# Forward and backward state steps of a chunked linear attention in one VectorE operation, on one core of a Trainium2 chip

## The chip, the core and the metric

The kernel runs on one core of one Trainium2 chip. The core has five engines that run their own queues in order and meet through semaphores: TensorE (PE in the profile, with its weight loads shown as PEld), VectorE (DVE), ScalarE (ACT), GpSimd (POOL) and SyncE (SP, which here only issues transfers). Matrix products go to PSUM, eight banks of 2 KB in each of 128 rows; everything else works in SBUF. The metric is the device time of one execution in microseconds (us), as the median of several runs.

## The reference

One layer of an encoder on x of 1024 positions by 1024 features, all in float32:

```python
h = rmsnorm(x, norm_mix_pre);  y = mixer(h, ...);      x = x + rmsnorm(y, norm_mix_post)
h = rmsnorm(x, norm_ffn_pre);  y = conv_mlp(h, ...);   x = x + rmsnorm(y, norm_ffn_post)
```

The mixer projects h once and splits the columns into a short convolution branch (y_a) and a gated linear attention (y_b) of four heads, with 64 key and 128 value features, run once forward and once backward over the positions. For one head and one direction, in chunks of 64 positions:

```python
cum = cumsum(log_a, within a chunk);  cum_last = cum at the chunk's end
q_in, k_in, k_out = q*exp(cum), k*exp(-cum), k*exp(cum_last - cum)
o_intra = mask(q_in @ k_in.T) @ v
kv      = k_out.T @ v                       # 64 x 128 for each of 16 chunks
state_(n+1) = exp(cum_last)_n * state_n + kv_n          # the chain over chunks
o       = o_intra + q_in @ state_n
```

The backward direction does the same on flipped inputs, with gates of its own. The outputs of both directions are added, normalised over each head's 128 features, multiplied with silu of a gate, joined with y_a and multiplied with w_out. conv_mlp is an up projection to 2 x 2816, a width-3 convolution over positions, a gated product and a down projection.

## The kernel before, in words

Weights and activations of the large products are split into a rounded part (names ending in h) and a remainder (l), and each product is three TensorE passes. Four of the large projections use a block scheme that needs seven block products in place of eight; its sums of weight blocks are made by GpSimd ahead of time, from rows of w_up and w_down that it loads itself, and are written back to DRAM (wud, wup, wdd) for the second half of the kernel. One such job is `up_begin`/`up_end` (tiles wu0 to wu3), `down_begin`/`down_end` (tiles wd0r, wd1r, ... two a job) or `pair_begin`/`pair_end` (wp4, wp5). A job's begin loads two tiles of 512 KB; its end makes four operations of 128x512 (L108 to L111, or L146 to L149, called sums in this text) and stores the tiles. `side()` takes the next job from a list: it begins it and ends what has been begun, all but the newest `ahead` jobs.

The order of work is that in which a scheduler lays out the program's operations; each engine then runs its list strictly in order. The part around the change is the attention heads, from 118 to 345 us of the span. There TensorE alternates between two kinds of work, head by head: projections of the convolution branch (pgc, pgv, pgb, 48 passes of 128x512 each) and of the next head's q and k (pqk), which keep it busy, and between them the attention products of one head: pko (the transpose of the decayed keys, tile `cum`), kv (k_out times v, L727), sc (scores, L708), po (outputs, L782 and L785) and pot (the transpose of the normalised outputs, L802). Between the passes of a projection, a list called `between` slips in pko, kv and sc of a head.

In SBUF, the first 64 rows of a head's tiles belong to the forward direction and the last 64 to the backward one: S (the states of 16 chunks, 128 columns each), dec (the decay of each chunk), qd, kin and cum. For a head:

- ScalarE copies kv from PSUM to S, four copies for each half of the chunks (L735 for the forward rows, L739 for the backward rows). The state that enters chunk c lies in S[:, c] for both directions, so the forward chain runs upward in c and the backward chain downward.
- `scan` then runs the chain on VectorE: 14 steps of 64 rows forward (`step_f`, L744) and 14 of 64 rows backward (`step_b`, L748), alternating in the middle. Its operations stand in VectorE's list together with the masking of the scores (L711, L715, giving A), the convolution branch (c, u, yT), the remainders of weights (L219), and the gates of the next head (m, cum, cl, L665 to L685).
- TensorE makes po in one PSUM tile of two banks: first 16 products of A with v, each with 64 rows and 64 output rows (L782), then 16 products of qd with S that take all 128 rows at once and so add both directions (L785).
- ScalarE squares po into `on` (L792), VectorE reduces it (L793), a few short operations make the factor, and VectorE multiplies po with it into `on` (L795). TensorE transposes `on` into pot, and VectorE writes yT (L803).

Between a head's reduce and the next head's kv copies, ScalarE's list holds the factor's two operations (L197, L199), a weight's rounding (L218), two copies of q (L651, L652) and the copy of pko to koT (L696), which the next kv products read.

PSUM tiles come from a pool of four tiles of two banks; a tile's first write waits for the last reader of the one that had its banks. The jobs' tiles come from a pool of eight (tag y) that also holds the yT tiles.

The main loop calls, for each head h, the attention's steps and the convolution's steps in turn, and `side()` once before the first head, and once after the heads 0 and 1.

Of the kernel before, what the change touches and what calls it, by code (L numbers as in the profile page):

```python
# [16 lines left out]
P = 128  # L17
# [23 lines left out]
def kernel(  # L41
# [39 lines left out]
    def ps_tile(name):  # L81
        return psp.tile([P, 1024], F32, tag="ps", name=name)
# [78 lines left out]

    begun, loads = [], []

    def side(tile=row_tile, after=None, ahead=0):


        if jobs:
            begin, end, i = jobs.pop(0)
            begun.append((end, i, begin(i, tile, after)))
        while len(begun) > ahead:  # L170
            end, i, t = begun.pop(0)
            with tc.issue_after(loads[-1].ins) if ahead else ExitStack():
                end(i, *t)

    NPB = 21
# [456 lines left out]


    S = mp.tile([P, NC, DV], F32, tag="S", name="S")
    nc.vector.memset(S[0:DK, 0, :], 0.0)
    nc.vector.memset(S[DK:P, NC - 1, :], 0.0)

    last_act = [None]
    left = []
    copied, gated = {}, [None]  # L640

    def gla_head(h):
# [31 lines left out]
        nc.vector.tensor_copy(cl[0:DK], cumv[0:DK, :, CH - 1])  # L674
        nc.vector.tensor_copy(cl[DK:P], cumv[DK:P, :, 0])
        s = 1.0 / 16.0
        nc.scalar.activation(dec, cl, AF.Exp, scale=s)
        kin = unit("kin", f"kin{h}")
        nc.scalar.activation(m, cum, AF.Exp, scale=s)
        nc.scalar.activation(kin, cum, AF.Exp, scale=-s)  # L680
# [36 lines left out]
        def states(i):  # L717
            b = i // 2
            if i % 2 == 0:
                tiles["kv"] = ps_tile(f"kv{h}_{b}")  # L720
            kv = tiles["kv"]
            for c8 in range(4 * (i % 2), 4 * (i % 2) + 4):
                t = b * 4 + c8 // 2
                par = c8 % 2
                r = slice(par * CH, (par + 1) * CH)
                o0 = par * HALF + (c8 // 2) * DV
                nc.tensor.matmul(kv[:, o0 : o0 + DV], tiles["koT"][r, t * P : (t + 1) * P], V[t][r, h * DV : (h + 1) * DV],  # L727
                                 start=True, stop=True)
            if i % 2 == 0:
                return  # L730
            kvv = kv.rearrange("p (a i d) -> p a i d", a=2, d=DV)
            for par in range(2):
                lo_c = b * 8 + par
                n = 4 if lo_c + 6 + 1 <= NC - 1 else 3
                nc.scalar.copy(S[0:DK, lo_c + 1 : lo_c + 1 + 2 * n - 1 : 2, :], kvv[0:DK, par, 0:n, :])  # L735
                i0 = 1 if lo_c == 0 else 0
                c0 = lo_c + 2 * i0
                n = 4 - i0
                last_act[0] = nc.scalar.copy(S[DK:P, c0 - 1 : c0 - 1 + 2 * n - 1 : 2, :], kvv[DK:P, par, i0:4, :])  # L739
            if b == 1:  # L740
                scan()

        def step_f(c):
            nc.vector.scalar_tensor_tensor(S[0:DK, c + 1, :], S[0:DK, c, :], dec[0:DK, c : c + 1], S[0:DK, c + 1, :],  # L744
                                           op0=ALU.mult, op1=ALU.add)

        def step_b(c):
            nc.vector.scalar_tensor_tensor(S[DK:P, c - 1, :], S[DK:P, c, :], dec[DK:P, c : c + 1], S[DK:P, c - 1, :],  # L748
                                           op0=ALU.mult, op1=ALU.add)

        def scan():
            for c in range(1, 8):
                step_f(c)
            for i in range(8, 15):
                step_b(NC + 6 - i)
                step_f(i)
            for c in range(7, 0, -1):
                step_b(c)

        def all_states():  # L760

# [6 lines left out]
        between.extend((decayed, lambda: None, all_states, lambda: None, lambda: [scores(i) for i in range(4)]))  # L768
        yield

        po = ps_tile(f"po{h}")

        for inner in (True, False):
            for c in range(NC) if inner else (c for g in range(0, NC, 4) for c in (g, g + 2, g + 1, g + 3)):
                t, par = divmod(c, 2)
                o0 = par * HALF + t // 2 * DV
                o = po[t % 2 * CH : (t % 2 + 1) * CH, o0 : o0 + DV]
                if inner:  # L780
                    r = slice(par * CH, (par + 1) * CH)
                    nc.tensor.matmul(o, A[r, t * CH : (t + 1) * CH], V[t][r, h * DV : (h + 1) * DV],  # L782
                                     start=t < 2, stop=False, skip_group_check=True)
                else:
                    nc.tensor.matmul(o, qd[:, c * CH : (c + 1) * CH], S[:, c, :], start=False, stop=True,  # L785
                                     skip_group_check=True)
        on = unit("sq", f"on{h}")
        ov = on.rearrange("p (t d) -> p t d", d=DV)
        ss = small.tile([P, NT], F32, tag="ssh", name=f"ssh{h}", bufs=2)

        with tc.high_priority() if h == 0 else ExitStack():
            nc.scalar.activation(on, po, AF.Square)  # L792
            nc.vector.reduce_sum(out=ss, in_=ov, axis=mybir.AxisListType.X)  # L793
            rs = rstd_of(ss, DV)
            nc.vector.tensor_mul(ov, po.rearrange("p (t d) -> p t d", d=DV), rs.unsqueeze(2).to_broadcast([P, NT, DV]))  # L795
        yield

        def outputs():
# [658 lines left out]
```

## Time and profile before

| | |
|---|---|
| median of 3 runs | 1069.47 us (1068.31 to 1071.57) |
| the profiled execution's own time | 1070.88 us |
| its span, first to last instruction | 1069.1 us, 14218 instructions |
| TensorE busy (matmul) | 1042.1 us (97%) |
| VectorE busy | 844.9 us (79%) |
| ScalarE busy | 480.0 us (45%) |
| GpSimd busy | 295.6 us (28%) |
| mean granted TensorE clock | 0.989 |

In a timeline row stand the start in us from the span's start, the time it took, engine, line and operation, then tiles and shapes as output<-input, the count of merged instructions, and in brackets the engine's idle time before it with what ended it. A row of merged instructions has the time from the first one's start to the last one's end. In the view of waits a row gives who waited, for whom, the total in us, how often, and the longest. In the view of stretches a row gives the stretch, its length, each engine's busy time with its number of instructions, the granted clock, the DMA share and GB/s.

### The profile page before, as it was taken

Reading aid. Unit: us, or ns where it says so; the run is one execution under the profiler, and the core shown is the slowest. Engines: PE = TensorE matmul, PEld = TensorE weight load, DVE = VectorE, ACT = ScalarE, POOL = GpSimd, SP = SyncE. Lnnn points to the kernel's source line nnn. Section 1 sums busy time; section 2 is a strip of 40 time slices with the busy share of each in tenths; the row PEclk is TensorE's granted clock in tenths of the full one; section 3 lists DMA queues with packets and bytes.
Section 4 is the critical chain, followed back from the end, with each engine's and each line's share of the span. In section 5 each row is a group of like instructions: output and inputs, shape, how many; then the busy total and the mean of one; then the engine's idle time right before and its main releaser. Section 6 shows DMA issues by size and latency. Waiting matters only on the chain.

```text
span 1069.1 us, 14218 instructions
## 1 busy us (share of the span) xinstructions
PE 1042.1 (97%) x5385; PEld 871.2 (81%) x5385; DVE 844.9 (79%) x1037; ACT 480.0 (45%) x664; POOL 295.6 (28%) x274
## 2 busy tenths in 40 slices
PE   8999996899999999999999999999999999999997
PEld 7987884788888888887888888888888888888886
DVE  6884679798878887999979877977987886655476
ACT  6552481545444334744534434344444455343443
POOL 1434485300006840001322423342240007600001
PEclk9999997899999999999999999999999999999999
DMA  9201665201247864344423323223333579977555
GB/s 303 100 20 45 192 229 185 79 21 40 60 128 243 288 248 148 99 129 158 138 75 122 118 69 128 99 89 109 109 105 102 193 266 342 357 253 233 176 163 212
DMA packets 126599, 165.02 MB, mean 154 GB/s; under 512 B 16177, under 2 KB 83906, under 8 KB 126530
## 3 DMA queue, kind: packets, MB, share of 16 engines
q1 hardware_dynamic: 114802, 121.90, 35.6%
q0 software_dynamic: 11152, 40.38, 10.3%
q10 hardware_dynamic: 576, 1.84, 0.4%
q8 instruction: 42, 0.69, 0.3%
q14 instruction: 27, 0.22, 0.1%
HBM read 117.68 MB, written 46.40 MB: 153 GB/s over the span
## 4 chain that ended last, share of the span: by engine, by line
PE 87%; DVE 8%; ACT 2%; DMA 1%; issue 1%; POOL 0%; SPq 0%; DVEq 0%; POOLq 0%; ACTq 0%
PE pb L311 16%; PE pc L311 11%; PE pdb L1325 10%; PE pa L311 9%; PE pw L933 8%; PE pgc L260 4%; PE pv L453 4%; PE pgv L260 3%; PE pqk L260 3%; PE pdd L1325 3%; PE pdc L1325 3%; PE pda L1325 3%; PE pgb L260 2%; DVE S L744 1%; PE pdl L1325 1%; PE pga L311 1%
## 5 line engine op out<-in xcount | busy, mean ns | idle before, releaser
L1325 PE MATMUL pdb<-d 128*128 128x512 f32 (+1 forms) x495 | 109.5, 382 | 0.0
L1325 PEld LDWEIGHTS pdb<-d 128*128 128x128 f32 x495 | 90.7, 188 | 18.0
L311 PE MATMUL pb<-t,uv 128*128 128x512 f32 x264 | 63.4, 389 | 0.0
L311 PEld LDWEIGHTS pb<-t,uv 128*128 128x128 f32 x264 | 49.5, 188 | 10.3
L1208 DVE TENSOR_TENSOR cg<-cv,pb 128x512 f32<-128x512 f32 x22 | 15.0, 684 | 35.3 <-PE pb L311 18.1
L1256 ACT ACTIVATE uu<-uu 128x1024 f32<-128x1024 f32 x22 | 23.4, 1062 | 35.9 <-DVE uu L1178 35.9
L744 DVE SCALAR_TENSOR_TENSOR S<-S,dec 64x128 f32<-64x128 f32 x56 | 28.0, 500 | 12.2 <-ACT S L735 10.5
L1214 ACT COPY cg<-pa 128x512 f32<-128x512 f32 x22 | 12.9, 587 | 47.0 <-PE pa L311 47.0
L1068 POOL TENSOR_TENSOR us61r<-uv6r 128x512 f32<-128x512 f32 x1 | 1.7, 1737 | 110.5 <-DVE cv L1236 110.5
L123 POOL COPY wp5g<-ident 128x1 f32<-128x1 f32 x1 | 0.2, 206 | 115.0 <-PE pgc L260 115.0
L1177 DVE SCALAR_TENSOR_TENSOR uv<-cv,prm,uv 128x1023 f32<-128x1023 f32 x22 | 31.9, 1448 | 0.0
L1325 PE MATMUL pdc<-d 128*128 128x512 f32 x132 | 30.1, 389 | 0.0
L1325 PE MATMUL pdd<-d 128*128 128x512 f32 x132 | 30.1, 389 | 0.0
L1325 PEld LDWEIGHTS pdd<-d 128*128 128x128 f32 x132 | 24.8, 188 | 5.1
L1325 PEld LDWEIGHTS pdc<-d 128*128 128x128 f32 x132 | 24.8, 188 | 5.1
L1178 DVE SCALAR_TENSOR_TENSOR uu<-cg,prm,uu 128x1023 f32<-128x1023 f32 x22 | 28.9, 1312 | 0.0
L1376 POOL DMA_DIRECT2D x2r<-x2d x4 | 2.1, 531 | 95.5 <-DMA d_8r<-actd 84.8
L946 ACT ACTIVATE tmp<-x 128x1024 f32<-128x1024 f32 x8 | 8.5, 1061 | 44.0 <-DVE x L943 44.0
L1178 DVE SCALAR_TENSOR_TENSOR uv<-cv,prm,uv 128x1023 f32<-128x1023 f32 x22 | 28.0, 1274 | 0.0
L1177 DVE SCALAR_TENSOR_TENSOR uu<-cg,prm,uu 128x1023 f32<-128x1023 f32 x22 | 28.0, 1274 | 0.0
L1259 DVE TENSOR_TENSOR uu<-uu,uv 128x1024 f32<-128x1024 f32 x22 | 27.2, 1237 | 0.0
L1176 ACT ACTIVATE uu<-cg,prm 128x1024 f32<-128x1024 f32 x22 | 25.2, 1143 | 3.1 <-ACT uv L1176 1.9
(1268 smaller groups left out, 3285.0 us busy)
## 6 DMA issues: line engine op xcount, KB each, us to landing
actd<-as SPq DMA_DIRECT2D x20, 512.0 KB, 2.7
x<-in_x_dram SPq DMA_DIRECT2D x16, 512.0 KB, 6.2
actd<-uu SPq DMA_DIRECT2D x10, 512.0 KB
x2d<-x SPq DMA_DIRECT2D x8, 512.0 KB, 3.1
actd<-uu SPq DMA_DIRECT2D x10, 256.0 KB, 2.0
out_dram<-o POOLq DMA_DIRECT2D x5, 512.0 KB, 6.1
x2r<-x2d POOLq DMA_DIRECT2D x4, 512.0 KB, 4.9
x2r<-x2d SPq DMA_DIRECT2D x4, 512.0 KB, 4.2
```

Of the source, the lines that this page charges most:

```text
L260: nc.tensor.matmul(o[hf], wt[:, k, :], act[hf][a][:, k, :], start=(k == 0 and wt is wh and a == 0), stop=(k == KT - 1 and wt is wl))
L311: nc.tensor.matmul(o, w[:, k, :], m[:, k, :], start=start and k == 0 and q == 0, stop=k == 3 and q == 2, skip_group_check=True)
L453: keep(nc.tensor.matmul(ps[:, n * 512 : n * 512 + VH], a[:, k, sl], w[:, k % 2, n * VH : (n + 1) * VH], start=(j == 0), stop=(j == 3 * KT ...
L744: nc.vector.scalar_tensor_tensor(S[0:DK, c + 1, :], S[0:DK, c, :], dec[0:DK, c : c + 1], S[0:DK, c + 1, :], op0=ALU.mult, op1=ALU.add)
L933: ins = nc.tensor.matmul(ps[:, n * HALF : (n + 1) * HALF], a[:, k, sl], w[:, n * HALF : (n + 1) * HALF], start=(i == 0 and q == 0), stop=( ...
L1176: nc.scalar.activation(u, src, AF.Copy, scale=ffn_tap(1, r))
L1177: nc.vector.scalar_tensor_tensor(u[:, 1:L], src[:, 0 : L - 1], ffn_tap(0, r), u[:, 1:L], op0=ALU.mult, op1=ALU.add)
L1178: nc.vector.scalar_tensor_tensor(u[:, 0 : L - 1], src[:, 1:L], ffn_tap(2, r), u[:, 0 : L - 1], op0=ALU.mult, op1=ALU.add)
L1208: nc.vector.tensor_add(cg[:, hi], cv[:, lo], pb)
L1256: last_act[0] = nc.scalar.activation(ug, ug, AF.Silu)
L1259: nc.vector.tensor_mul(ug, ug, uv)
L1325: nc.tensor.matmul(o, a[:, 0, sl], b[:, 1, r], start=start and i == 0, stop=stop and i == 2, skip_group_check=True)
```

## The change

Four edits belong together.

1. The backward states are stored in S in reverse: the state that enters chunk c in the backward chain lies in S[64:128, 15 - c], and dec's backward half is reversed too (by a second ScalarE operation). Both chains then run upward, and one VectorE operation on 128 rows makes one step of both: 14 operations a head in place of 28. The zero that starts both chains is written by one operation.
2. Forward and backward states of one chunk no longer lie in the same column of S, so a product over 128 rows cannot take both. The products of qd with S are split: 16 for one half of the rows and 16 for the other, each with 64 rows. Together with the 16 products of A with v that makes 48 in three turns. The products that read rows 0 to 63 add into one PSUM tile (po...f), those that read rows 64 to 127 into another (po...b).
3. The evacuation adds the two: ScalarE copies the second tile to `on`, VectorE adds the first, ScalarE squares `on` into the first tile's banks, VectorE reduces from there, and the final product is made in place in `on`.
4. `side` takes a `hold`. In heads 0 and 1 GpSimd first copies one column of the last state (S[:, 15]) to a small tile (turn), and the ends of the jobs that are due stand behind that copy in its list. The call before the first head falls away; the job of wd2r and wd3r (wd1 in the prediction; the job of wd0r and wd1r is wd0 there) is only begun after head 0 and ends after head 1's steps, as do wp4's sums.

```diff
-    def side(tile=row_tile, after=None, ahead=0):
+    def side(tile=row_tile, after=None, ahead=0, hold=None):
...
-            with tc.issue_after(loads[-1].ins) if ahead else ExitStack():
+            with tc.issue_after(loads[-1].ins) if ahead else tc.issue_after(hold.ins) if hold else ExitStack():
                 end(i, *t)
...
-        nc.scalar.activation(dec, cl, AF.Exp, scale=s)
+        nc.scalar.activation(dec[0:DK], cl[0:DK], AF.Exp, scale=s)
+        nc.scalar.activation(dec[DK:P], cl[DK:P, ::-1], AF.Exp, scale=s)
...
-                c0 = lo_c + 2 * i0
+                c1 = NC - lo_c - 6
                 n = 4 - i0
-                last_act[0] = nc.scalar.copy(S[DK:P, c0 - 1 : c0 - 1 + 2 * n - 1 : 2, :], kvv[DK:P, par, i0:4, :])
+                last_act[0] = nc.scalar.copy(S[DK:P, c1 : c1 + 2 * n - 1 : 2, :],
+                                             kvv[DK:P, par, i0:4, :][:, ::-1, :])
             if b == 1:
-                scan()
...
+                for c in range(1, NC - 1):
+                    stepped[0] = nc.vector.scalar_tensor_tensor(S[:, c + 1, :], S[:, c, :], dec[:, c : c + 1],
+                                                                S[:, c + 1, :], op0=ALU.mult, op1=ALU.add)
...
-        po = ps_tile(f"po{h}")
+        po = [ps_tile(f"po{h}{x}") for x in "fb"]
...
+        for turn in range(3):
+            for c in range(NC):
                 t, par = divmod(c, 2)
...
+                d = par ^ (turn == 2)
+                r = slice(d * DK, (d + 1) * DK)
+                bank = (d, par, t % 2)
+                if turn == 0:
+                    w, v = A[r, t * CH : (t + 1) * CH], V[t][r, h * DV : (h + 1) * DV]
                 else:
+                    w, v = qd[r, c * CH : (c + 1) * CH], S[r, NC - 1 - c if d else c, :]
+                nc.tensor.matmul(out_of(c, d), w, v, start=bank not in seen, stop=turn > 0, skip_group_check=True)
...
-            nc.scalar.activation(on, po, AF.Square)
-            nc.vector.reduce_sum(out=ss, in_=ov, axis=mybir.AxisListType.X)
+            nc.scalar.copy(on, po[1])
+            nc.vector.tensor_add(on, on, po[0])
+            nc.scalar.activation(po[0], on, AF.Square)
+            nc.vector.reduce_sum(out=ss, in_=po[0].rearrange("p (t d) -> p t d", d=DV), axis=mybir.AxisListType.X)
...
     next(gla[0])
-    side()
     next(fill)
...
         next(fill)
+        if h < 2:
+
+            turn = small.tile([P, 1], F32, tag="ss", name=f"turn{h}")
+            side(hold=nc.gpsimd.tensor_copy(turn, S[:, NC - 1, 0:1]))
...
-        if h < 2:
-            side()
+        if h == 0:
+            side(ahead=1)
```

How GpSimd's list moves around head 0's steps. Before, from the last sum of wu2 on:

```order
L111 TENSOR_TENSOR wu2g<-wu2g 128x512
L108 TENSOR_TENSOR wu3v<-wu3v 128x512
L116 DMA wud<-wu2g 128x2x512
L140 DMA wd0r<-in_w_down_dram 128x1024
L109 TENSOR_TENSOR wu3v<-wu3g,wu3v 128x512
L140 DMA wd1r<-in_w_down_dram 128x1024
L110 TENSOR_TENSOR wu3g<-wu3v,wu3g 128x512
L115 DMA wud<-wu3v 128x2x512
L111 TENSOR_TENSOR wu3g<-wu3g 128x512
L146 TENSOR_TENSOR wd0r<-wd0r 128x512
```

and now:

```order
L111 TENSOR_TENSOR wu2g<-wu2g 128x512
L116 DMA wud<-wu2g 128x2x512
L140 DMA wd0r<-in_w_down_dram 128x1024
L140 DMA wd1r<-in_w_down_dram 128x1024
L851 COPY turn_1592<-S 128x1
L108 TENSOR_TENSOR wu3v<-wu3v 128x512
L146 TENSOR_TENSOR wd0r<-wd0r 128x512
L109 TENSOR_TENSOR wu3v<-wu3g,wu3v 128x512
L147 TENSOR_TENSOR wd0r<-wd1r,wd0r 128x512
L110 TENSOR_TENSOR wu3g<-wu3v,wu3g 128x512
L115 DMA wud<-wu3v 128x2x512
```

The eight sums of wu3 and wd0 stand behind the copy that reads the last state; the loads of wd0r and wd1r stay ahead of it.

VectorE's list of head 0 from the masking on. Before:

```order
L715 TENSOR_TENSOR A_1460<-Am 128x512
L748 SCALAR_TENSOR_TENSOR S<-S,dec_1313 64x128
L818 TENSOR_TENSOR c_1396<-c_1396,pgv_1467 128x1024
L748 SCALAR_TENSOR_TENSOR S<-S,dec_1313 64x128
L219 TENSOR_TENSOR gc1l<-gc1r,gc1h 128x1024
L748 SCALAR_TENSOR_TENSOR S<-S,dec_1313 64x128
L821 SCALAR_TENSOR_TENSOR u_1618<-c_1396,prm,u_1618 128x1023
L748 SCALAR_TENSOR_TENSOR S<-S,dec_1313 64x128
L822 SCALAR_TENSOR_TENSOR u_1618<-c_1396,prm,u_1618 128x1023
L665 TENSOR_SCALAR m_1630<-pg_1627,prm 128x1024
```

and now:

```order
L715 TENSOR_TENSOR A_1444<-Am 128x512
L744 SCALAR_TENSOR_TENSOR S<-S,dec_1312 128x128 x5
L813 TENSOR_TENSOR c_1380<-c_1380,pgv_1451 128x1024
L219 TENSOR_TENSOR gc1l<-gc1r,gc1h 128x1024
L664 TENSOR_SCALAR m_1618<-pg_1615,prm 128x1024
L816 SCALAR_TENSOR_TENSOR u_1588<-c_1380,prm,u_1588 128x1023
L667 TENSOR_TENSOR m_1618<-m_1618,cum_1619 128x1024
L817 SCALAR_TENSOR_TENSOR u_1588<-c_1380,prm,u_1588 128x1023
L668 SCALAR_TENSOR_TENSOR cum_1619<-rst,m_1618 64x1024
L669 SCALAR_TENSOR_TENSOR cum_1619<-rst,m_1618 64x1024
```

The last steps stand together ahead of the convolution branch, which before was woven with backward steps; lines below L634 have numbers smaller by one in the changed kernel, and those from L744 on shift by more. Further down in VectorE's list, the reduce of head 0 moves from ahead of the last product of the next head's gates to behind it. Before:

```order
L681 TENSOR_TENSOR cum_1631<-cl_1639,cum_1631 128x1024
L684 TENSOR_TENSOR kin_1644<-kin_1644,kd_1455 128x1024
L219 TENSOR_TENSOR gv1l<-gv1r,gv1h 128x1024
L793 TENSOR_REDUCE ssh_1743<-on_1742 128x8
L685 TENSOR_TENSOR cum_1631<-cum_1631,kd_1455 128x1024
L198 TENSOR_SCALAR rv<-ssh_1743,eps 128x8
```

and now:

```order
L681 TENSOR_TENSOR cum_1619<-cl_1627,cum_1619 128x1024
L684 TENSOR_TENSOR kin_1633<-kin_1633,kd_1439 128x1024
L219 TENSOR_TENSOR gv1l<-gv1r,gv1h 128x1024
L685 TENSOR_TENSOR cum_1619<-cum_1619,kd_1439 128x1024
L786 TENSOR_TENSOR on_1748<-on_1748,po0f 128x1024
L788 TENSOR_REDUCE ssh_1749<-po0f 128x8
L198 TENSOR_SCALAR rv<-ssh_1749,eps 128x8
```

The add of the two output tiles (L786) is new and stands between. TensorE's list keeps its order but for the 48 products in the place of 32.

More of the change, by code (lines that the diff above doesn't have):

```diff
@@ L634 @@
     S = mp.tile([P, NC, DV], F32, tag="S", name="S")
-    nc.vector.memset(S[0:DK, 0, :], 0.0)
-    nc.vector.memset(S[DK:P, NC - 1, :], 0.0)
-    last_act = [None]
+    nc.vector.memset(S[:, 0, :], 0.0)
+    last_act, stepped = [None], [None]
     left = []
@@ L736, in states @@
                 i0 = 1 if lo_c == 0 else 0
-                c0 = lo_c + 2 * i0
+                c1 = NC - lo_c - 6
                 n = 4 - i0
-                last_act[0] = nc.scalar.copy(S[DK:P, c0 - 1 : c0 - 1 + 2 * n - 1 : 2, :], kvv[DK:P, par, i0:4, :])
+                last_act[0] = nc.scalar.copy(S[DK:P, c1 : c1 + 2 * n - 1 : 2, :],
+                                             kvv[DK:P, par, i0:4, :][:, ::-1, :])
             if b == 1:
-                scan()
[L743 to L758, printed above, removed]
+                for c in range(1, NC - 1):
+                    stepped[0] = nc.vector.scalar_tensor_tensor(S[:, c + 1, :], S[:, c, :], dec[:, c : c + 1],
+                                                                S[:, c + 1, :], op0=ALU.mult, op1=ALU.add)
         def all_states():
@@ L769, in gla_head, with out_of @@
         yield
-        po = ps_tile(f"po{h}")
-        for inner in (True, False):
-            for c in range(NC) if inner else (c for g in range(0, NC, 4) for c in (g, g + 2, g + 1, g + 3)):
-                t, par = divmod(c, 2)
[L778 to L783, printed above, removed]
-                else:
-                    nc.tensor.matmul(o, qd[:, c * CH : (c + 1) * CH], S[:, c, :], start=False, stop=True,
-                                     skip_group_check=True)
+        po = [ps_tile(f"po{h}{x}") for x in "fb"]
+        def out_of(c, d):
+            t, par = divmod(c, 2)
+            o0 = par * HALF + t // 2 * DV
+            return po[d][t % 2 * CH : (t % 2 + 1) * CH, o0 : o0 + DV]
+        seen = set()
+        for turn in range(3):
+            for c in range(NC):
+                t, par = divmod(c, 2)
+                d = par ^ (turn == 2)
[3 more added lines that the diff above has]
+                    w, v = A[r, t * CH : (t + 1) * CH], V[t][r, h * DV : (h + 1) * DV]
+                else:
+                    w, v = qd[r, c * CH : (c + 1) * CH], S[r, NC - 1 - c if d else c, :]
+                nc.tensor.matmul(out_of(c, d), w, v, start=bank not in seen, stop=turn > 0, skip_group_check=True)
+                seen.add(bank)
         on = unit("sq", f"on{h}")
@@ L791, in gla_head @@
         with tc.high_priority() if h == 0 else ExitStack():
-            nc.scalar.activation(on, po, AF.Square)
-            nc.vector.reduce_sum(out=ss, in_=ov, axis=mybir.AxisListType.X)
+            nc.scalar.copy(on, po[1])
+            nc.vector.tensor_add(on, on, po[0])
+            nc.scalar.activation(po[0], on, AF.Square)
+            nc.vector.reduce_sum(out=ss, in_=po[0].rearrange("p (t d) -> p t d", d=DV), axis=mybir.AxisListType.X)
             rs = rstd_of(ss, DV)
-            nc.vector.tensor_mul(ov, po.rearrange("p (t d) -> p t d", d=DV), rs.unsqueeze(2).to_broadcast([P, NT, DV]))
+            nc.vector.tensor_mul(ov, ov, rs.unsqueeze(2).to_broadcast([P, NT, DV]))
         yield
```

## The prediction

> **What bounds the kernel now.** I read the chain of waits first, then TensorE's own waits, then three stretches that hold the same work.
>
> The chain of the page (part 4), by engine:
>
> ```profile
> PE 87%; DVE 8%; ACT 2%; DMA 1%; issue 1%; POOL 0%; SPq 0%; DVEq 0%; POOLq 0%; ACTq 0%
> ```
>
> TensorE sets the end for most of the span, so a change is worth what it takes from the 8% in which VectorE (DVE) stands on the path. TensorE's waits between 118 and 345 us, the attention heads:
>
> ```profile
> PE po L785 <- DVE S L748: 5.5, 1, 5.5
> PE po L782 <- DVE A L715: 5.2, 1, 5.2
> PE pko L694 <- DVE rv L198: 3.2, 1, 3.2
> ```
>
> Three waits, once each, all in head 0; heads 1 to 3 have none. The busy-time view over the same 149 TensorE instructions, from a head's `po` products to the next head's `kv` products, for heads 0, 1 and 2:
>
> ```profile
> 167.30:207.50 40.20, 26.36 (x147) 21.73 (x146) 36.27 (x39) 13.70 (x16) 18.13 (x16) 0.75 0.45 143
> 229.30:249.20 19.90, 19.90 (x149) 16.65 (x148) 17.74 (x21) 11.67 (x14) 0.00 (x0) 1.00 0.15 39
> 270.90:290.80 19.90, 19.90 (x148) 16.66 (x147) 17.95 (x20) 9.56 (x12) 0.00 (x0) 1.00 0.25 75
> ```
>
> The columns are the stretch, its length, then busy time of PE, PEld, DVE, ACT and POOL, and the granted clock. Head 0 takes 40.2 us for what takes 19.9: 13.9 us of waits, the rest at a clock of 0.75. So at most 20.3 us can be won. GpSimd (POOL) works 18.1 us in that stretch and none in the others; VectorE's steps show why that matters (tile S on VectorE, head 0 and head 1):
>
> ```profile
> 150.50:181.00 30.50, 21.55 (x28) 0.85 0.61 213
> 210.40:223.60 13.20, 9.74 (x28) 1.00 0.00 1
> ```
>
> The same 28 steps cost 21.55 us beside GpSimd and 9.74 without it, 0.35 each. The first of head 0 in the timeline, and the first and last of the seven GpSimd sums that run with them:
>
> ```profile
> 150.51 11.35 DVE L744 SCALAR_TENSOR_TENSOR S<-S,dec 64x128 f32<-64x128 f32 x7 [5.97 <-ACT S L735]
> 161.90 1.81 DVE L748 SCALAR_TENSOR_TENSOR S<-S,dec 64x128 f32<-64x128 f32 x1
> ```
> ```profile
> 151.41 1.29 POOL L109 TENSOR_TENSOR wu3v<-wu3g,wu3v 128x512 f32<-128x512 f32 x1
> ...
> 162.25 1.30 POOL L149 TENSOR_TENSOR wd1r<-wd1r 128x512 f32<-128x512 f32 x1
> ```
>
> Eight steps take 13.16 us in place of 2.8: 10.4 us over seven sums, 1.48 us a sum. VectorE is busy from there until head 1's `cum` is ready at 200.1, and TensorE waits for it.
>
> **The change, part by part.** *The steps.* 56 steps of 128 rows replace 112 of 64. A step's price on 128 rows is not in the trace; bounds are 0.35, if rows cost nothing, and 0.70, if they cost in proportion; I take 0.35, since a copy of 64 rows,
>
> ```profile
> 246.93 1.23 DVE L653 COPY kd<-pqk 64x1024 f32<-64x1024 f32 x1
> ```
>
> lasts as long as the 128-row L685 further down (1.21), both of 1024 columns. That is 4.9 us a head instead of 9.74, and in head 0 instead of 21.55, since order puts the sums behind the last step. But the first step now needs the backward half of the last chunk group, so it waits for the last of ScalarE's eight copies of S:
>
> ```profile
> 152.78 0.58 ACT L739 COPY S<-kv 64x512 f32<-64x512 f32 x1
> ```
> ```profile
> 212.71 0.58 ACT L739 COPY S<-kv 64x512 f32<-64x512 f32 x1
> ```
>
> It starts at 153.4, not 150.5: +2.9 (the same in head 1, 213.3 for 210.4).
>
> *The sums.* They are not saved. The eight of wu3 and wd0 now follow head 0's steps and meet the operations queued there; the eight of wd1 and wp4 move from head 0 to behind head 1's steps. Contended rows of head 0's stretch, and the same lines in head 1, where GpSimd is idle:
>
> ```profile
> 174.81 2.24 DVE L219 TENSOR_TENSOR gc1l<-gc1r,gc1h 128x1024 fp32r<-128x1024 f32 x1
> ...
> 188.53 1.09 DVE L674 COPY cl<-cum 64x16 f32<-64x16 f32 x1
> ...
> 192.13 2.31 DVE L681 TENSOR_TENSOR cum<-cl,cum 128x1024 f32<-128x1024 f32 x1
> 194.36 2.31 DVE L684 TENSOR_TENSOR kin<-kin,kd 128x1024 f32<-128x1024 f32 x1
> ...
> 197.73 1.21 DVE L793 TENSOR_REDUCE ssh<-on 128x8 f32<-128x1024 f32 x1
> 198.86 1.21 DVE L685 TENSOR_TENSOR cum<-cum,kd 128x1024 f32<-128x1024 f32 x1
> ```
> ```profile
> 232.05 0.17 DVE L674 COPY cl<-cum 64x16 f32<-64x16 f32 x1
> ...
> 233.21 1.23 DVE L683 TENSOR_TENSOR qd<-qd,m 128x1024 f32<-128x1024 f32 x1 [0.79 <-ACT m L679]
> 234.35 1.22 DVE L681 TENSOR_TENSOR cum<-cl,cum 128x1024 f32<-128x1024 f32 x1
> ```
> ```profile
> 187.70 1.90 POOL L108 TENSOR_TENSOR wp4v<-wp4v 128x512 f32<-128x512 f32 x1 [2.46 <-DMA wp4v<-in_w_up_dram]
> ...
> 193.90 1.70 POOL L111 TENSOR_TENSOR wp4g<-wp4g 128x512 f32<-128x512 f32 x1
> ```
>
> The four sums of wp4 cost `cl` 0.92 and L681 and L684 1.09 each: 3.1 us, 0.78 a sum, and one of the four nothing. So a sum's price lies between 0 and 1.48 us; I take 0.8, from the long operations, since those are what the sums now meet.
>
> The Trainium skill (SBUF — State Buffer, section "SBUF: two separate sides") says that VectorE operations with two SBUF inputs and GpSimd share one port pair, locked for a whole instruction, so that the other fully blocks. The trace agrees in kind; by that rule each sum could cost its whole 1.29 us, and the sum of this prediction would come out near 1073, the first rival's case.
>
> *Head 0 added up.* Head 1's `cum` (L685) ended at 200.1. Start +2.9; steps 21.55 to 4.9, -16.7; the contended rows at their free length (1.02 + 0.92 + 1.09 + 1.09), -4.1; the reduce (L793), which order now puts behind L685, -1.2; eight held sums at 0.8, +6.4: 187.4. TensorE's side:
>
> ```profile
> 166.80 0.61 PE L260 MATMUL pgb<-hTh,gb0l 128*128 128x512 f32 x2
> ...
> 172.60 1.99 PE L782 MATMUL po<-V,A 64*64 64x128 f32 x32 [5.18 <-DVE A L715]
> ```
> ```profile
> 229.26 1.10 PE L782 MATMUL po<-V,A 64*64 64x128 f32 x32
> 230.30 1.97 PE L785 MATMUL po<-S,qd 128*64 128x128 f32 x32
> 232.19 0.73 PE L260 MATMUL pqk<-hTh,qk3h 128*128 128x512 f32 x2
> ...
> 244.57 1.03 PE L694 MATMUL pko<-ident,cum 128*128 128x128 f32 x8
> ...
> 249.17 2.06 PE L727 MATMUL kv<-V,koT 64*128 64x128 f32 x32
> ```
>
> It reaches `po` at 167.3. The 14 steps (4.9 us from 153.4) and the masking among them, for which I allow 2.5 us, are done by 161, so the first two waits go with 6 us to spare. From `po` to `pko` is 15.3 us in head 1, so it reaches `pko` at 182.8 and waits 4.6 us for `cum`. After that the longest leg is the new evacuation:
>
> ```profile
> 195.44 1.01 ACT L792 ACTIVATE on<-po 128x1024 f32<-128x1024 f32 x1
> ...
> 198.98 0.30 ACT L197 ACTIVATE rs<-ssh,eps 128x8 f32<-128x8 f32 x1 [2.53 <-DVE ssh L793]
> ...
> 202.42 1.01 ACT L696 COPY koT<-pko 128x1024 f32<-128x1024 f32 x1
> ```
>
> Add (as L685, 1.2), Square (1.0) and reduce (1.2) end at 190.9; from L197's start to the end of the koT copy is 4.45, so `kv` starts at 195.4, not 207.5: **-12.1**. A slow clock after the wait is covered by that leg:
>
> ```profile
> 200.22 1.94 PE L694 MATMUL pko<-ident,cum 128*128 128x128 f32 x8 [3.17 <-DVE rv L198]
> ...
> 206.57 1.04 PE L802 MATMUL pot<-ident,on 128*128 128x128 f32 x8
> ```
>
> even at this pace, 6.35 us where head 1 has 3.6 (a loss of 2.7), `pko` to `pot` would end at 193.8.
>
> *TensorE's extra products.* 48 with 64 rows replace 16 and 16. The first 16 of head 1 take 1.04 us; if 32 more keep that pace, 3.1 us against 2.9, +0.2 a head, +0.6 over heads 1 to 3 (head 0's lies before a wait). Bound above: the pace of L785, 1.89/16 = 0.118 each, +1.9 a head.
>
> *The other edits.* The second dec operation (as short as `cl`, 0.17) and the copy of po's second bank (as Square, 1.0 us) lie on ScalarE, busy 13.7 of 40.2 us in head 0's row and 11.7 of 19.9 in head 1's, while VectorE works on `cum`; uncovered they would cost 1.2 a head. In head 0 `pgc` now takes the bank that the yT0 product frees, which waits for wu3v's held store; by order it precedes `cum`, whose lateness is counted already.
>
> *Head 1.* ScalarE's next koT copy
>
> ```profile
> 245.98 1.02 ACT L696 COPY koT<-pko 128x1024 f32<-128x1024 f32 x1
> ```
>
> ends 2.2 us before `kv` needs it. Later start +2.9, steps -4.9, add +1.2, wait for Square +1.0, reduce behind one more operation by order +1.2: the reduce comes 1.4 us later, TensorE 0.2 later, slack 1.0. Of the eight moved sums, wp4's four must first wait for a load (as their row above shows), so I count six before the reduce: 4.8, of which the 0.8 that L683 waits for `m` is hidden: 4.0 - 1.0 = **+3.0**.
>
> Sum: -12.1 + 3.0 + 0.6 = -8.5 us. The profiled execution took 1070.88 (span 1069.1 and 1.8 around it), 1.4 above the median of the three runs, 1069.47: 1062.4 by the one, **1061** by the other, on which the rivals' times stand too.
>
> **The rivals.**
> 1. *The moved sums cost more than the steps save.* Place: head 1's reduce and koT copy, where `kv` waits. At 1.48 a sum head 0 gains only 6.7, and head 1 loses 11.8 - 0.8 - 1.0 = 10.0 and 2.7 at a slow clock: with the 0.6 of TensorE +6.6, 1076. It decides from about 1.1 us a sum. For it: the steps paid 1.48. Against: steps are short and dependent, the operations there long, wp4's paid 0.78.
> 2. *The sums find gaps.* At 0 a sum `cum` is ready at 181.0, TensorE never waits, and head 0 gets all 20.3 us less 0.8: 1050, and up to 1056 with some of it left. For it: one of wp4's sums cost nothing beside L835 and L683. Against: 3 of 4 cost 0.9 to 1.1.
> 3. *The half-array products do not overlap by rows.* 1.7 more in each of heads 1 to 3: 1066. Against: the first turn has the same pattern and does 16 in 1.04.
> 4. *The sums are not held.* Then 14 steps still stand beside seven sums, 4.9 + 10.4 = 15.3 us in place of 21.55, +2.9 for the start: some -3.6, 1066. Against: order.
>
> The Trainium skill (TensorEngine Tiling (Array Packing), "Restrictions and Gotchas") says that different row tiles cannot access one PSUM bank at the same time. No row here shows that, as each half here has a bank of its own before and after; by it rival 3 is unlikely, and the sum stays.
>
> **How the numbers follow.** Forecast 0.62 (own range 1056 to 1066), rival 1 0.12, rival 2 0.15, rival 3 0.08, rival 4 0.03. Within 0.3% is 1066.3 to 1072.7, about what three runs can tell from no change. Faster: 0.57 + 0.15 + 0.02 + 0.01 = 0.75; slower: 0.10 of rival 1 and 0.01; the rest 0.14. The range 1053 to 1069 leaves out rival 1 and the far end of rival 2.
>
> **What would show it.** Steps of 0.35 us at 128 rows, 14 in some 5 us from 153.4 on, with no sum among them; no wait of `po`; a wait of `pko` of 3 to 6 us in head 0; sums right behind the steps of heads 0 and 1, lengthening L219, the scans and L681; a wait of 1 to 5 us at `pot` or `kv` in head 1; `po` at 3.1 us a head. Wrong: a step near 0.7 us, `po` near 5 us, or a wait in head 1 over 9 us.

## The result, and the profile after

The changed kernel took 1062.80 us (median of 4 runs, 1061.24 to 1063.34) beside 1070.08 us for the kernel before, a ratio of 0.993 with a 95% interval of 0.9911 to 0.9949: 7.3 us faster. A second series of runs gave 1063.22 beside 1070.72, ratio 0.9932 (0.9917 to 0.9947). The profiled execution took 1063.34, with a span of 1061.6, 7.5 less than that of before.

The chain of the page and TensorE's waits between 118 and 345 us, in the changed kernel:

```profile
PE 86%; DVE 8%; ACT 2%; issue 1%; DMA 1%; POOL 0%; SPq 0%; DVEq 0%; ACTq 0%; POOLq 0%
```
```profile
PE pot L797 <- DVE on L790: 3.8, 2, 3.2
PE pko L694 <- DVE cum L685: 2.9, 1, 2.9
PE kv L727 <- ACT koT L696: 0.7, 1, 0.7
PE kv L727 <- ACT kd L653: 0.4, 1, 0.4
```

In the rounded shares of the chain a gain of 0.7% does not show; the waits show where it lies. The two waits of `po` are gone. `pko` waits 2.9 us in head 0; `pot`, which did not wait before, waits 0.7 us in head 0 and 3.2 us in head 1. The stretches from `po` to the next head's `kv`, for heads 0, 1 and 2 (columns as in the prediction: PE, PEld, DVE, ACT, POOL, granted clock):

```profile
167.10:193.50 26.40, 22.12 (x179) 17.80 (x178) 24.63 (x22) 10.88 (x14) 14.87 (x13) 0.94 0.48 160
215.90:239.90 24.00, 20.84 (x179) 17.32 (x178) 21.30 (x21) 11.91 (x15) 10.91 (x9) 0.94 0.32 110
263.50:283.30 19.80, 19.80 (x179) 16.68 (x178) 15.49 (x18) 10.63 (x14) 0.00 (x0) 1.00 0.18 55
```

Head 0 fell from 40.2 to 26.4 us, head 1 rose from 19.9 to 24.0, and head 2 is as it was. GpSimd now works in both of the first two stretches, and the clock is below 1 in both. Laid side by side instruction by instruction, TensorE reaches the work behind head 0's `kv` products at 196.19 in place of 209.52 (13.3 earlier), and that behind head 1's at 243.66 in place of 251.15 (7.5 earlier). From there on the two traces run in parallel to the end. So head 0 gave 13.3 us and head 1 took 5.8 back.

VectorE's steps by tile S, heads 0 and 1, and the operations that follow head 0's steps, with the sums beside them:

```profile
153.10:160.20 7.10, 4.89 (x14) 1.00 0.39 133
199.60:206.50 6.90, 4.88 (x14) 1.00 0.00 0
```
```profile
160.07 1.21 DVE L813 TENSOR_TENSOR c<-c,pgv 128x1024 f32<-128x1024 f32 x1
...
162.71 1.27 DVE L664 TENSOR_SCALAR m<-pg,prm 128x1024 f32<-128x1024 f32 x1
163.91 2.37 DVE L816 SCALAR_TENSOR_TENSOR u<-c,prm,u 128x1023 f32<-128x1023 f32 x1
166.21 2.30 DVE L667 TENSOR_TENSOR m<-m,cum 128x1024 f32<-128x1024 f32 x1
...
177.28 1.09 DVE L673 COPY cl<-cum 64x16 f32<-64x16 f32 x1
...
184.29 1.22 DVE L685 TENSOR_TENSOR cum<-cum,kd 128x1024 f32<-128x1024 f32 x1
```
```profile
160.28 0.18 POOL L851 COPY turn<-S 128x1 f32<-128x1 f32 x1 [7.34 <-DVE S L744]
160.42 1.28 POOL L108 TENSOR_TENSOR wu3v<-wu3v 128x512 f32<-128x512 f32 x1
161.68 2.26 POOL L146 TENSOR_TENSOR wd0r<-wd0r 128x512 f32<-128x512 f32 x1
```

Fourteen steps of 0.35 us each run undisturbed from 153.16 to 160.15, the sums start right behind them, and `cum` ends at 185.5. The sums lengthen L816 and L667 by 1.1 us each, and the small copy L673 from 0.17 to 1.09, but not L813 and L664, which lie beside sums too: each of those two reads a PSUM tile (pgv, pg). The sums are lengthened as well: the one of wd0r above takes 2.26 us where a free one takes 1.28.

In head 1 the other eight sums meet the convolution branch:

```profile
225.06 2.31 DVE L219 TENSOR_TENSOR gc2l<-gc2r,gc2h 128x1024 fp32r<-128x1024 f32 x1
227.30 2.31 DVE L816 SCALAR_TENSOR_TENSOR u<-c,prm,u 128x1023 f32<-128x1023 f32 x1
229.64 2.19 DVE L817 SCALAR_TENSOR_TENSOR u<-c,prm,u 128x1023 f32<-128x1023 f32 x1
231.76 1.21 DVE L786 TENSOR_TENSOR on<-on,po1f 128x1024 f32<-128x1024 f32 x1
234.06 1.23 DVE L788 TENSOR_REDUCE ssh<-po1f 128x8 f32<-128x1024 f32 x1 [1.09 <-ACT po1f L787]
```
```profile
224.78 1.52 POOL L108 TENSOR_TENSOR wp4v<-wp4v 128x512 f32<-128x512 f32 x1 [3.06 <-DMA wp4v<-in_w_up_dram]
...
231.29 1.70 POOL L111 TENSOR_TENSOR wp4g<-wp4g 128x512 f32<-128x512 f32 x1
```
```profile
238.07 1.94 PE L797 MATMUL pot<-ident,on 128*128 128x128 f32 x8 [3.16 <-DVE on L790]
239.95 3.79 PE L727 MATMUL kv<-V,koT 64*128 64x128 f32 x32
```

Three of wp4's sums cost 1.1, 1.0 and 0.9 us; the fourth, beside L786, costs nothing, and L786 reads PSUM (po1f). The factor is then late, `pot` waits 3.16 us, and it and `kv` run at half clock: 1.94 and 3.79 us, where the kernel before needs 1.03 and 2.06 in this head. That is 2.6 us on top of the wait.

### The profile page after: what moved, and what is told of

Read it like the earlier page. It is cut to its first block, busy times and chain, and to the rows that moved or that the text cites. A ratio compares the mean times of both kernels' runs of the same rounds, so it can differ in the third digit from the quotient of the medians.

```text
span 1061.6 us, 14441 instructions
## 1 busy us (share of the span) xinstructions
PE 1040.9 (98%) x5513; PEld 870.0 (82%) x5513; DVE 819.4 (77%) x984; ACT 485.2 (46%) x672; POOL 304.2 (29%) x276
## 4 chain that ended last, share of the span: by engine, by line
PE 86%; DVE 8%; ACT 2%; issue 1%; DMA 1%; POOL 0%; SPq 0%; DVEq 0%; ACTq 0%; POOLq 0%
PE pb L311 16%; PE pc L311 11%; PE pdb L1323 10%; PE pa L311 9%; PE pw L931 8%; PE pv L453 4%; PE pgc L260 4%; PE pgv L260 3%; PE pdd L1323 3%; PE pdc L1323 3%; PE pda L1323 3%; PE pqk L260 2%; PE pgb L260 2%; PE pdl L1323 1%; PE pga L311 1%
## 5 line engine op out<-in xcount | busy, mean ns | idle before, releaser
L744 DVE SCALAR_TENSOR_TENSOR S<-S,dec 128x128 f32<-128x128 f32 x56 | 19.6, 350 | 23.9 <-ACT S L740 22.6
L944 ACT ACTIVATE tmp<-x 128x1024 f32<-128x1024 f32 x8 | 8.5, 1061 | 46.7 <-DVE x L941 46.7
L1085 ACT COPY cv<-pa 128x512 f32<-128x512 f32 x22 | 12.8, 587 | 29.4 <-PE pa L311 29.4
```

The costliest lines, as they stand in the source:

```text
L744: stepped[0] = nc.vector.scalar_tensor_tensor(S[:, c + 1, :], S[:, c, :], dec[:, c : c + 1], S[:, c + 1, :], op0=ALU.mult, op1=ALU.add)
```

## The experiments

Times are medians; ratios are to the kernel before, run beside it.

| kernel | us | ratio, 95% interval |
|---|---|---|
| the change, second series | 1063.22 | 0.9932 (0.9917 to 0.9947) |
| sums held, steps as before | 1068.53 | 0.9983 (0.9973 to 0.9993) |
| joined steps, sums not held | 1066.78 | 0.9968 (0.9958 to 0.9978) |
| the change, head 1's sums later | 1058.42 | 0.9895 (0.9882 to 0.9909) |
| the change without the 16 sums | 1051.98 | 0.9840 (0.9827 to 0.9854) |
| the change, products half by half | 1067.41 | 0.9966 (0.9952 to 0.9979) |
| the change, 12 sums later | 1054.98 | 0.9850 (0.9833 to 0.9867) |
| steps as before, 12 sums later | 1057.62 | 0.9874 (0.9859 to 0.9889) |

The theory: the gain comes from taking GpSimd's sums from beside the steps and from halving the steps; the loss is what the moved sums cost elsewhere. Rivals: one of the two parts earns it all; the loss comes from the longer evacuation or from the 48 products.

### The hold alone

The kernel before, with the sums held behind head 0's and head 1's last steps (both chains' ends are copied); dots stand for lines left out:

```diff
-    side()
     next(fill)
...
+        if h < 2:
+            turn = small.tile([P, 1], F32, tag="ss", name=f"turn{h}")
+            nc.gpsimd.tensor_copy(turn[0:DK], S[0:DK, NC - 1, 0:1])
+            side(hold=nc.gpsimd.tensor_copy(turn[DK:P], S[DK:P, 0, 0:1]))
...
-        if h < 2:
-            side()
+        if h == 0:
+            side(ahead=1)
```

> The kernel before, with the sums held as in the change, but with its own 28 steps of 64 rows, its own products and its own evacuation. Theory (the hold earns most of it, the joined steps the rest): the steps start at 150.5 us and cost 0.35 each with no sum beside them; the rest of VectorE's work up to cum is that of the changed kernel (185.4 there, from a start at 153.2 with 14 steps). So 2.7 earlier, 4.9 more for steps, 1.2 more for the reduce that stands ahead: cum at about 188.8, pko waits about 6 us in head 0, head 0 gains about 10 in place of 13.3, head 1 again loses 5 to 6: about 1065, ratio 0.995. Rival (the hold alone is the whole gain): 1063 or less, ratio 0.993 or lower. Rival (without the joined steps the hold earns nothing): 1070.

Measured 1068.53, a gain of 1.7 us: the theory's 1065 was 3.5 us off, the first rival's 1063 more, and the result lies nearest to the rival by which the hold alone earns nothing, though just clear of it. Its steps (tile S in VectorE's busy time), the place where it stalls, the store of wu3v ahead of that, and TensorE's wait:

```profile
150.00:175.00 25.00, 9.74 (x28) 1.00 0.27 85
```
```profile
167.01 0.35 DVE L748 SCALAR_TENSOR_TENSOR S<-S,dec 64x128 f32<-64x128 f32 x1
...
182.98 1.22 DVE L835 TENSOR_TENSOR yT<-u,pgb 128x1024 f32<-128x1024 f32 x1 [2.96 <-issue]
```
```profile
179.72 0.74 POOL L115 DMA_DIRECT2D wud<-wu3v  x1
```
```profile
PE pko L694 <- DVE rv L198: 9.2, 1, 9.2
```

The 28 steps cost their free 9.74 us, as expected. But the last one is woven into the convolution branch and runs at 167.0, so the sums start 7.3 us later than in the changed kernel. The yT0 product (L835) takes its tile from the pool in which wu3v lay, and starts 3.3 us after wu3v's store was issued, having stood idle for 2.96 us; `pko` then waits 9.2 us in place of 2.9. That the store is what it waited for is inferred from the dependency, since the trace names no releaser here; in the last experiment, where that store is issued at 173.3, the idle time is gone. In the profiled execution (1067.56) head 0 gained 8.4 us, and head 1 lost 4.8 of them. So with eight sums and their stores behind it the hold is worth little where it hangs on a last step that stands far down VectorE's list. The joined steps have that effect too, and the prediction did not price it apart: they end early, and what is held behind them starts early.

### The joined steps alone

The changed kernel with the calls of `side` where they stood before, without a hold.

```diff
     next(gla[0])
+    side()
...
-            side(hold=nc.gpsimd.tensor_copy(turn, S[:, NC - 1, 0:1]))
...
-        if h == 0:
-            side(ahead=1)
+        if h < 2:
+            side()
```

> The changed kernel without the hold: GpSimd's sums stand where they stood before, beside head 0's steps. Theory: the 14 steps cost 4.9 us plus 1.48 for each of the sums that runs in their time, some 7 to 15 us in place of 7; seven sums at most run beside them. cum in head 0 ends at 192 to 197 where it ended at 200.1 before, kv starts 3 to 8 us earlier than 207.5, head 1 loses nothing: 1063 to 1067, ratio 0.994 to 0.997. Rival (joined steps are worth nothing under the sums, because the sum and not the count of steps sets the price): 1069 to 1071, ratio 0.999 to 1.001.

Measured 1066.78, a gain of 3.4 us, as the theory and the prediction's fourth rival (some -3.6) had it. Tile S in VectorE's busy time, the first seven steps, and two of TensorE's waits:

```profile
150.00:175.00 25.00, 13.35 (x14) 0.93 0.69 225
```
```profile
153.35 11.12 DVE L744 SCALAR_TENSOR_TENSOR S<-S,dec 128x128 f32<-128x128 f32 x7 [8.85 <-ACT S L740]
```
```profile
PE po0b L778 <- DVE c L813: 2.2, 1, 2.2
PE pgc L260 <- DVE yT L830: 2.0, 1, 2.0
```

Seven steps take 11.12 us where they take 2.68 free: 8.4 us over the six sums that run meanwhile, 1.41 a sum, as before the change (1.48). The price goes with the sums that run meanwhile and not with the number of steps, so under the sums joined steps save only their own time. The two waits are new and come from the second output tile: it takes the banks of pgv, and pgc those of pgb, so lateness of VectorE's c and yT now reaches TensorE directly. Alone the two parts give 1.7 and 3.4 us, together 7.3 to 7.5. Neither is the whole; that together they give more than their sum of 5.1 is at the edge of what the intervals can tell, each of which reaches 1 us or more to either side.

### Head 1's sums later

In the changed kernel, wd1's four sums go behind a copy that reads head 0's `on` after its last product (L790 of the change), wp4's four behind the same of head 1.

```diff
-        if h < 2:
+        if h == 0:
             turn = small.tile([P, 1], F32, tag="ss", name=f"turn{h}")
...
+        if h == 0:
+            side(ahead=1)
         next(gla[h])
+        if h < 2:
+            turn = small.tile([P, 1], F32, tag="ss", name=f"late{h}")
+            side(hold=nc.gpsimd.tensor_copy(turn, normed[h][:, 0:1]), more=False)
```

> The changed kernel, with wd1's four sums held behind head 0's last product of the evacuation (the one that writes on with the factor), and wp4's four behind head 1's, where VectorE then waits for ScalarE's copies of kv. Theory (the eight sums beside the convolution branch of head 1 cost it 3.2 us of waiting at pot and 2.6 us of a slow clock after it): head 1's wait goes, 5.8 us come back, up to 1 us is lost at head 0's copy kd, which now meets sums: 1057 to 1058, ratio 0.988. Rival (head 1's wait comes from the longer evacuation, copy, add and Square, and not from the sums): 1062 to 1063, ratio 0.993.

Measured 1058.42, 0.4 above the theory's 1057 to 1058 and far from the rival's time: no wait of TensorE is left in head 1, though its copy, add and Square are unchanged. Its reduce starts 28.8 us after head 1's first step, against 34.4 in the changed kernel, so the eight sums had cost 5.6 us. The expected loss at the copy kd did not come. The sum and the copy that run together:

```profile
233.55 1.29 POOL L108 TENSOR_TENSOR wp4v<-wp4v 128x512 f32<-128x512 f32 x1
```
```profile
233.57 1.23 DVE L653 COPY kd<-pqk 64x1024 f32<-64x1024 f32 x1
```

Both have their free length: the copy reads PSUM (pqk).

### No held sums

```diff
     def up_end(k, ag, av):
-        block_sums(ag, av)
+        if k < 3:
+            block_sums(ag, av)
```

and the same for `pair_end` (c > 4) and `down_end` (q > 1). This kernel leaves work out: its second half multiplies with weights that lack these sums, so its time is a bound and not an alternative.

> The changed kernel without the 16 held sums: wu3, wd0, wd1 and wp4 are written back as they were loaded, so that the second half works on other weights. Theory (all that is left of the loss is the price of these sums, and the slow clock that their waits bring): VectorE's operations behind the steps fall back to 1.2 us each, cum of head 1 ends at 180 to 181, before TensorE asks for it at 182.6; no wait of 1 us is left in heads 0 to 2; 12.8 us beyond the changed kernel: about 1050, ratio 0.981. Rival (the 48 products, the copy and the add cost time of their own, as would show in heads that no sum disturbs): 1053 to 1056.

Measured 1051.98, 10.8 us below the changed kernel's 1062.80; the theory had 12.8. The last product of the gates and TensorE's `pko` in head 0:

```profile
178.83 1.22 DVE L688 TENSOR_TENSOR cum<-cum,kd 128x1024 f32<-128x1024 f32 x1
```
```profile
182.64 1.04 PE L697 MATMUL pko<-ident,cum 128*128 128x128 f32 x8
```

`cum` is ready at 180.05, and `pko` does not wait. With its steps 0.3 us later than the changed kernel's, this puts the price of head 0's eight sums at 185.51 - 180.05 + 0.3 = 5.8 us, 0.72 each. In the changed kernel VectorE's operations on the way to `cum` are lengthened by 6.5 us in all, 0.81 a sum; the difference is hidden, because without the sums VectorE waits 0.78 us for ScalarE's `m`. The only waits left in the head are together a wait of 1.1 us of `kv` for ScalarE, behind the longer evacuation. The time lies between the theory's 1050 and the rival's 1053, but the trace leaves the rival little: heads 1 to 3 show no wait at all, and `po` takes 2.85 us in each head.

### The products of one half of the rows first

```diff
-        for turn in range(3):
-            for c in range(NC):
+        for side_d in range(2):
+            for turn, c in [(0, 2 * t + side_d) for t in range(NT)] + [(1 if c % 2 == side_d else 2, c) for c in range(NC)]:
```

> The changed kernel with its 48 output products in another order: first the 24 that read rows 0 to 63, then the 24 that read rows 64 to 127. Theory (the 48 cost no more than the 32 of before because four quarters of the array work at once, two by rows and two by columns): with one half of the rows at a time two quarters are left, po takes 5.3 us a head in place of 2.85. Heads 2 and 3 lose 2.5 each, in heads 0 and 1 it lies before a wait for VectorE: 1066 to 1068. Rival (products of 64 rows do not overlap by rows, as the third rival of the prediction had it): po stays at 2.85 and the time at 1062.8.

Measured 1067.41, within the theory's 1066 to 1068. `po` of head 2 fills this stretch of TensorE's busy time, of this kernel and then of the changed one:

```profile
262.70:268.00 5.30, 5.30 (x98) 1.00 0.02 3
```
```profile
263.50:266.40 2.90, 2.90 (x98) 2.71 (x97) 1.95 (x3) 2.17 (x4) 0.00 (x0) 1.00 0.02 6
```

The same 48 products take 5.2 us when only one half of the rows works, 2.85 when both halves take turns. So row halves do overlap, and the third rival falls. One output tile for both halves, which would make copy and add needless, was not tried; no run here shows whether products of different row halves may write one bank.

### Twelve sums later, with joined steps and without

Only wu3's four sums stay behind head 0's steps; wd0's, wd1's and wp4's are held behind the evacuations of heads 0, 1 and 2. First in the changed kernel:

```diff
-        if h < 2:
+        if h == 0:
...
-            side(hold=nc.gpsimd.tensor_copy(turn, S[:, NC - 1, 0:1]))
+            side(ahead=1, hold=nc.gpsimd.tensor_copy(turn, S[:, NC - 1, 0:1]))
...
         next(gla[h])
+        if h < 3:
+            turn = small.tile([P, 1], F32, tag="ss", name=f"late{h}")
+            side(hold=nc.gpsimd.tensor_copy(turn, normed[h][:, 0:1]), more=False)
...
-        if h == 0:
+        if h < 2:
             side(ahead=1)
```

> The changed kernel, with only wu3's four sums behind head 0's steps; wd0's four are held behind head 0's last product of the evacuation, wd1's behind head 1's, wp4's behind head 2's. Theory (a sum costs about 0.6 us where VectorE's chain to cum runs and little where VectorE waits for ScalarE's copies): cum in head 0 ends 2 to 3 us earlier than 185.4, pko waits under 1 us at full clock, kv starts at 188.5 to 190; up to 1 us a head is lost at the copies kd: 1053.5 to 1056, ratio 0.986. Rival (a sum costs the same wherever it is put): as the one before with eight late sums, 1058.4.

Measured 1054.98, 8.2 us below the changed kernel and the best of the kernels that make all the sums. `cum` ends 3.4 us earlier, at 182.1, and `pko` waits no more. All of TensorE's waits in the heads:

```profile
PE pot L799 <- DVE on L791: 2.3, 1, 2.3
PE kv L728 <- ACT koT L697: 0.7, 1, 0.7
PE kv L728 <- ACT kd L654: 0.4, 1, 0.4
```

All three lie in head 0; the largest is that of the evacuation, whose add stands behind `cum` in VectorE's list. Here, too, the late sums cost TensorE nothing. wd0's first two lie beside kd and yT, which keep their free length (1.23 and 1.28 us); its last two lie where VectorE is idle. wp4's do lengthen two operations of VectorE in head 2, by 1.0 and 0.9 us, without a wait of TensorE:

```profile
189.35 1.26 POOL L146 TENSOR_TENSOR wd0r<-wd0r 128x512 f32<-128x512 f32 x1
```
```profile
189.37 1.23 DVE L653 COPY kd<-pqk 64x1024 f32<-64x1024 f32 x1
...
271.07 2.31 DVE L818 SCALAR_TENSOR_TENSOR u<-c,prm,u 128x1023 f32<-128x1023 f32 x1
```

Then the same places in the kernel before, with 28 steps, 32 products and the short evacuation:

```diff
-    side()
     next(fill)
...
         if h == 0:
+            turn = small.tile([P, 1], F32, tag="ss", name=f"turn{h}")
+            nc.gpsimd.tensor_copy(turn[0:DK], S[0:DK, NC - 1, 0:1])
+            side(ahead=1, hold=nc.gpsimd.tensor_copy(turn[DK:P], S[DK:P, 0, 0:1]))
...
+        if h < 3:
+            turn = small.tile([P, 1], F32, tag="ss", name=f"late{h}")
+            side(hold=nc.gpsimd.tensor_copy(turn, normed[h][:, 0:1]), more=False)
...
         if h < 2:
-            side()
+            side(ahead=1)
```

> The kernel before, with 28 steps of 64 rows, its own products and evacuation, and the sums held in the late places: wu3's behind head 0's last backward step, wd0's, wd1's and wp4's behind the evacuation products of heads 0, 1 and 2. Theory (the joined steps are worth their 4.9 us on VectorE less the 2.9 of the later start, and more where the last step stands far down the list): the last step ends at 167, cum at 186 to 188, pko waits 4 to 6 us in head 0 and none elsewhere: 1057 to 1060, 2 to 4 above the changed kernel with the same late sums. Rival (once the sums are away, later start and longer evacuation cancel what the joined steps save): within 1 us of that kernel.

Measured 1057.62; its only wait in the heads:

```profile
PE pko L695 <- DVE rv L198: 4.7, 1, 4.7
```

So with the sums in good places the joined steps are worth 2.6 us, at the lower end of what the theory expected, and the places of the sums are worth 13 us without touching a step, which is more than the whole change gave.

### The change once more

> The changed kernel once more, as the measure for the runs beside it: 1062 to 1063.5, ratio 0.993. If the slow clock behind the 3.2 us wait of pot in head 1 depends on where in time the wait falls, this profile may show pot and kv at their free 1.1 and 2.7 us (then some 2.6 us less in the span) in place of 1.9 and 3.8.

Measured 1063.22. In the profiled execution of this series head 1 took back 3.9 us in place of 5.8 (span 1059.4, 9.7 less than before):

```profile
236.91 1.55 PE L797 MATMUL pot<-ident,on 128*128 128x128 f32 x8 [2.05 <-DVE on L790]
238.66 3.03 PE L727 MATMUL kv<-V,koT 64*128 64x128 f32 x32 [0.20 <-ACT koT L696]
```

The wait was 1.1 us shorter, and the slow clock reached less far into `kv` (3.03 in place of 3.79). The shorter wait has a cause in the rows: wp4's first sum, which waits for its load, started 0.16 us behind L219, where in the first profile it started 0.28 us ahead of it (224.78 and 225.06).

```profile
224.99 1.22 DVE L219 TENSOR_TENSOR gc2l<-gc2r,gc2h 128x1024 fp32r<-128x1024 f32 x1
```
```profile
225.15 2.20 POOL L108 TENSOR_TENSOR wp4v<-wp4v 128x512 f32<-128x512 f32 x1 [3.61 <-DMA wp4v<-in_w_up_dram]
```

This time L219 kept its free length and the sum was lengthened; in the first profile it was L219 that paid (2.31). So the two executions of one kernel differ by some 2 us in this place alone, and here the one that started second paid.

## Why the prediction was right, and where it was off

The forecast was 1061, with an own range of 1056 to 1066; measured were 1062.8 and 1063.2, and on profiles -7.5 and -9.7 us where the sum had -8.5. The sum is right in total, but its terms were off in both directions (head 0 by -1.2, head 1 by +2.8, the products by -0.6), so that part of the closeness is luck.

- **Steps.** 14 of 0.35 us on 128 rows, from 153.4 on, 4.9 us a head: measured 153.16 and 4.89. That rows cost nothing was right.
- **Head 0.** -12.1 expected, -13.3 measured. `cum` came at 185.5 in place of 187.4, the wait of `pko` was 2.9 in place of 4.6, and `kv` started at 193.5 in place of 195.4. The durations came out as they were added up: from the first step to the end of `cum`, VectorE's operations take 48.75 us before and 33.26 in the changed kernel, -15.5 where the sum had -15.6, with 0.81 for each of the eight sums. What the sum left out are the seams. Before, steps stood between the long operations, and VectorE idled for about 0.03 us on each side of a step (L219 ends at 177.05, the next step starts at 177.08); now long operations stand side by side, and their records overlap by about 0.08 us (L816 ends at 166.28, L667 starts at 166.21). That makes 1.7 us; the steps' earlier start makes 0.2. That no `po` would wait was right.
- **Head 1.** This is the term that was mis-sized: +3.0 expected, 5.8 and 3.9 measured. The mechanism was the one named, wd1's and wp4's sums ahead of the reduce, and the wait came out as long as forecast (3.16 us in the first profile), but by errors that cancel. Six sums paid, as counted, though for another reason: all eight end before the reduce at 234.06, and two of them cost nothing, beside operations that read PSUM (`m<-pg` and L786). The six cost 5.6 us (0.93 each) where the sum had 4.0, because it took 0.8 as hidden behind L683's wait for `m`, and that wait is still there (0.78 us). Against that, the evacuation left 2.4 us before TensorE needed `on` (with the sums late, L791 ends at 232.40 and `pot` starts at 234.81), where the sum had 1.0. The miss itself is the clock: the slow stretch behind the wait of `pot` cost 2.6 and 1.5 us, and the prediction had it for `pko` in head 0 (where it saw it covered) and for head 1 only in the first rival.
- **TensorE's products.** +0.6 expected; `po` takes 2.85 us a head where it took 3.0: -0.15 a head. Forty-eight products that use four quarters of the array in turn cost no more than 16 of them and 16 over all rows.
- **The other edits** were covered in head 0, except that the longer evacuation shows up wherever `cum` is early: 2.3 us at `pot` in the kernel with twelve late sums.
- **The rivals.** The first (sums cost more than the steps save) had place and mechanism right and the price wrong: it decides from 1.1 us a sum, and they paid 0.72 to 0.81 in head 0 and, in head 1, 0.93 for each of six. The second did not come true in the change, where the sums found few gaps; with twelve sums in later places 1054.98 lies in its range. The third fell in the reordering of the products. The fourth was measured by itself: -3.4 us where it had -3.6; its own terms (21.55 - 15.3 - 2.9) give -3.35.

The prediction took an average price for a sum, between one that cost nothing and ones that cost 1.1, and did not ask why one of the four of wp4 was free. The traces suggest the reason by the operands. In all traces of kernels that make the sums, between 118 and 345 us, no operation of VectorE that reads a PSUM tile was lengthened beside a sum (kd 1.23, m<-pg 1.27, c<-c,pgv 1.21, yT<-pot 1.28), while those with two inputs in SBUF took mostly 2.2 to 2.4 in place of 1.2 or 1.3 (lines 219, 816 and 681 of the changed kernel, for example). That held for different kernels and places, but no run changed an operand and nothing else. The late places have both, operations that read PSUM and idle time of VectorE; no run separates the two.

The Trainium skill (SBUF — State Buffer, section "Who interferes with whom") states that division, with a condition: an operation with at most one SBUF input, outside the two-port modes, does not contend with GpSimd, and one with two SBUF inputs contends with a GpSimd instruction that reads SBUF. The traces agree, with the numbers above, for kd, c and yT on the one side and m<-m,cum, u and the remainders on the other. The copy `cl<-cum` has one SBUF input and still took 1.09 us beside a sum in place of 0.17; the section counts copies among the operations that can enter a two-port mode, and no run shows in which mode this one ran.

## What to carry to other kernels

Work that is moved out of one engine's way lands in another's: price it at the place where it lands, operation by operation and by operands, and not by its average. Beside GpSimd's sums, VectorE's operations that read PSUM ran free and those with two SBUF inputs mostly paid about 1 us each, so the stretch behind an evacuation, with such operations and idle time, was a better place than the one right behind the steps. What is held behind a marker starts when the marker does, so the marker's place in its engine's list, and the stores that follow late, belong in the sum.

## What the runs showed of the hardware

Waits of the same length had different ends. In the changed kernel `pot` waited 3.16 us, and the granted clock fell to half for about 7 us; with the hold alone, it waited 3.18 us, and the clock stayed at 1. TensorE's stretches around the two (busy time, granted clock), and the second kernel's rows:

```profile
238.00:240.00 2.00, 1.93 (x10) 0.50 0.02 4
```
```profile
242.00:244.00 2.00, 0.82 (x8) 1.00 0.46 188
```
```profile
243.18 1.06 PE L802 MATMUL pot<-ident,on 128*128 128x128 f32 x8 [3.18 <-DVE on L795]
244.18 1.16 PE L727 MATMUL kv<-V,koT 64*128 64x128 f32 x16
```

A second pair is shorter: in head 0 `pot` waited 2.28 us with twelve late sums and then ran at its free 1.06 us, and 2.27 us with the products half by half, where the clock fell to 0.50 and `pot` took 1.94. The length of the wait alone does not decide it: a wait of 2.05 us in the second profile of the change was also followed by a slow stretch (0.50). The Trainium skill (TensorE: Matmul & The Clock Gate, Part 1) says that the clock falls after an idle window of about 3.4 us that runs freely, without regard to the kernel. That the outcome varies between equal waits agrees with a free-running window; that 2.05 us was enough does not agree with a whole idle window of that length. No run here varied the phase by itself, so the cause stays open.
